# Two-layer trunk on one core: where the residual sum at each layer's end is made (matrix unit with the identity, scalar engine and GpSimd, in place of vector engine adds)

## The chip, the cores and the metric

The kernel runs on 1 core of one Trainium2 chip. The metric is the device time of one execution in microseconds (us); three runs of the kernel before gave a median of 1525.57 us. Engines are called as the profile calls them: PE is TensorE, DVE is VectorE, ACT is ScalarE, POOL is GpSimd, SP is SyncE; PSUM is PE's output memory of 8 banks, each 128 rows of 512 f32 values.

## The reference, cut to what matters

```python
D_MODEL, SEQ, DEPTH, N_EXPERTS, TOP_K = 1024, 512, 2, 16, 2
ALPHA = (2.0 * DEPTH) ** 0.25

def moe(x, ...):
    e_idx, gates = route(xf, w_router, b_router)      # top 2 of 16 experts per token
    ...
    hb = jax.nn.silu(xb @ w1[e]) * (xb @ w3[e])       # one expert on its tokens
    y = (hb @ w2[e]) * gate
    out = jnp.zeros((t, d), x.dtype).at[tok_s].add(y) # two shares per token
    return out.reshape(bsz, seq, d)

for layer in range(DEPTH):
    m = conv_mixer(x, ...) if layer % 2 == 0 else rglru_mixer(x, ...)
    x = layer_norm(ALPHA * x + m, ln1_g[layer], ln1_b[layer])
    f = moe(x, w_router, b_router, moe_w1[layer], moe_w3[layer], moe_w2[layer])
    x = layer_norm(ALPHA * x + f, ln2_g[layer], ln2_b[layer])
```

The change lies in the last line, `layer_norm(ALPHA * x + f)`, which is run twice: at the end of layer 0 (here "the first end", about 704 to 755 us into the execution) and at the end of layer 1 ("the last end", from about 1460 us to the end of the program).

## The kernel before, in words

The 512 tokens are four tiles of 128 rows (`NT` = 4), each row 1024 wide. Every weight matrix is brought in raw pieces (`raw`, 1 MB each) and split for PE into a high part `wh` (ACT, L137) and a low part `wl` (DVE, in places POOL, L148); a product is then three matmuls, high by high, high by low and low by high (L305). An expert runs w1, w3 and w2 in four steps each. Between w3 and w2 its hidden rows are transposed on PE in two halves (L271, `turn(0)` and `turn(1)`); each half is taken out of its bank as a high part `ht0h`, `ht1h` (ACT, L418) and a low part `ht0l`, `ht1l` (DVE, L421).

All engines work through their own queues in the order in which the code is written, and that order is written out by hand in `moe`. `ws.later` collects the low parts of the weight piece that is taken meanwhile, and `ws.lows()` writes them: for the last expert this puts the low part of the piece for w2(1) as four 128x512 instructions on DVE between `ht0l` and `ht1l`.

The experts before the last one scatter their gated rows to DRAM, two shares per token (`yd`). The last expert doesn't. Its end runs like this:

- `base_begin`, in the last expert's w1: POOL's queue loads for each tile t the rows of x (`az`, 512 KB, L1486) and the two stored shares (`ay`, 1 MB, L1488). The `az` of two tiles share one buffer. Behind the eight loads POOL adds the two shares, one 128x1024 add for each tile (L1491).
- `base_sum(t)`: DVE makes `az = ALPHA * az + ay` (128x1024, L1496): tile 0 between the two last `wl` pieces, tiles 1 to 3 behind `yl`.
- w2 gives two halves of 512 columns: w2(0) and w2(1) the first, w2(2) and w2(3) the second. `share(h)` takes half h out, times the gate, as `yh` (ACT, L1502) and `yl` (DVE, L1503).
- `total_mm(t, h)`: PE puts the last expert's rows at their tokens' places in a bank, by two matmuls with the one-hot matrix `place` (L1509).
- `total_half(t, h)`: DVE adds the bank to `az` (128x512, L1516) and takes the norm's statistics of the sum (`bn_stats`, L1517).
- `total(t)` does the second half so and then the moments: two small DVE instructions (L547, L548) and the power -1/2 on POOL (L549).

Then, at the first end, ACT normalises each tile (L1676, after a small DVE instruction, L1673), PE transposes it (L563) and DVE takes the transposes out (L577), which is the input of layer 1's first product. At the last end ACT normalises (L1768), gain and bias are put on by POOL for columns 0 to 383 and by DVE for the rest (L1772, L1773), and the rows leave by SP's queue.

Lines to follow in the code: L1480 to L1491 (`base_begin`), L1493 to L1497 (`base_sum`), L1506 to L1522, and the last expert's part of `moe`.

Of the kernel before, what the change touches and what calls it, by code (L numbers as in the profile page):

```python
# [15 lines left out]
AF = mybir.ActivationFunctionType  # L16
OP = mybir.AluOpType
AX = mybir.AxisListType

P = 128  # L20
T = 512
NT = T // P
# [7 lines left out]
ALPHA = 4.0 ** 0.25  # L30
# [317 lines left out]
class Trunk:  # L348
# [1002 lines left out]
    def moe(self, layer, loaded):  # L1351

        nc, tc, ws = self.nc, self.tc, self.ws
        v = nc.vector
        slots, hot = {}, []

        def aux(q):
            return lambda t: self.aux[:, t, q]

        def fill(qs, hot):  # L1360
            slots.update(zip(qs, self.slot_rows(hot, [aux(q) for q in qs], [q in SMALL for q in qs])))

        hot0 = self.one_hot(self.pos[:, :, 0])
        first = self.slot_rows([hot0], [aux(0)], [False], ())
        rows = self.R("in", "xe")
        nc.gpsimd.memset(rows, 0.0)
        xe = self.gather((first[0][:, 0:1],), False, rows)
        ws.lows()
        self.rank()
        ws.open, ws.total, ws.cap = True, True, 32  # L1370
        ws.pump()
        nxt = Block(self, ws, plain=True)
        nxt.rows_in(xe)
        self.choice()
        self.placed()
        nxt.w1(0)
        hot = [self.one_hot(self.pos[:, :, q], v, q in SMALL) for q in (1, 2, 3)]
        nxt.rest()
        nxt.w1(1)
        self.gates_out()  # L1380
        nxt.w1(2)
        nxt.w1(3)
        slots[0], = self.slot_rows([hot0], [aux(0)], [False], first)
        fill([1, 2, 3], hot)
        hot = []
        xe = self.gather(slots[1], 1 in SMALL, rows)
        for e in range(E):
            cur, last = nxt, e == E - 1
            if e < 12:
                q = e // 4 * 4 + 4 + 2 * (e % 4)  # L1390
                if e % 4 < 2:
                    hot += [self.one_hot(self.pos[:, :, i], nc.gpsimd, i in SMALL) for i in (q, q + 1)]
                if e % 4 == 2:
                    q = e // 4 * 4 + 4
                    fill(list(range(q, q + 4)), hot)
                    hot = []
            if e == E - 2:
                ws.cap = 16
            if e:
                cur.w1(1)  # L1400
                cur.w1(2)
                if last:
                    self.base_begin()
                cur.w1(3)
            cur.w3(0)
            if e == 1:
                self.extra_blocks()
            if e == 4:
                self.nextra = nc.values_load(self.ni[0:1, 0:1], min_val=0, max_val=32)
            cur.w3(1)  # L1410
            cur.w3(2)
            if not last:
                nxt = Small(self, ws) if e + 1 in SMALL else Block(self, ws, 4 if e == E - 2 else 2)
                nxt.rows_in(xe)
                if e + 2 < E:
                    xe = self.gather(slots[e + 2], e + 2 in SMALL, rows)
            ws.later = []
            cur.w3(3)
            cur.turn(0)
            ws.lows()  # L1420
            if last:
                cur.turn(1)
            else:
                nxt.w1(0, ws.next(), lambda h: h or cur.turn(1))
                ws.ahead()
            cur.w2(0)
            if last:
                loaded()
                self.base_sum(0)
            cur.w2(1)  # L1430
            if e == E - 2:
                self.place_rows(slots[E - 1][0])
            if last:
                break
            cur.w2(2)
            cur.w2(3)
            self.scatter(cur.ys, slots.pop(e), cur.small, ROOM[e])
            if e == E - 2:
                with tc.If(self.nextra > 0):  # L1439
                    it = self.S([P, 1], F32, "it", bufs=1)  # L1440
                    nc.vector.memset(it, 0.0)
                    self.kept = {}
                    with tc.For_i(0, self.nextra, 1):
                        self.extra(layer, it)
                    self.kept = None
        gate = slots[E - 1][1]
        self.share(0, cur.ys[0], gate)
        for t in (1, 2):
            self.base_sum(t)
        ws.lead = 1  # L1450
        cur.w2(2)
        self.base_sum(3)
        ws.lead = 0
        for t in range(NT):
            self.total_mm(t, 0)
        cur.w2(3)
        for t in range(2):
            self.total_half(t, 0)
        self.share(1, cur.ys[1], gate)
        for t in range(2):  # L1460
            self.total_mm(t, 1)
        for t in range(2, NT):
            self.total_half(t, 0)
            self.total_mm(t, 1)
        ws.total, ws.open, ws.cap = False, False, 10
        ws.lead = 4
        ws.later = []
        ws.ahead()
# [11 lines left out]
    def base_begin(self):  # L1480

        nc = self.nc
        self.bz, self.bp, self.yhl, self.bst = [], {}, {}, {}
        for t in range(NT):
            z = self.V([P, D], F32, "az")
            nc.gpsimd.dma_start(z, self.x1d[t * P:(t + 1) * P])  # L1486
            y = self.V8([P, 2, D], F32, "ay")
            nc.gpsimd.dma_start(y, self.yd[2 * t * P:2 * (t + 1) * P].rearrange("(p k) d -> p k d", k=2))  # L1488
            self.bz.append((z, y))
        for _, y in self.bz:  # L1490
            nc.gpsimd.tensor_tensor(y[:, 0], y[:, 0], y[:, 1], op=OP.add)  # L1491

    def base_sum(self, t):  # L1493

        z, y = self.bz[t]
        self.nc.vector.scalar_tensor_tensor(z, z, ALPHA, y[:, 0], op0=OP.mult, op1=OP.add)  # L1496
        self.bz[t] = z  # L1497

    def share(self, h, ps, gate):
# [3 lines left out]
        self.nc.vector.scalar_tensor_tensor(lo, ps, gate, hi.bitcast(F32), op0=OP.mult, op1=OP.subtract)  # L1503
        self.yhl[h] = (hi, lo)

    def total_mm(self, t, h):  # L1506
        ps = self.bp[t, h] = self.bank()
        for i, q in enumerate(self.yhl[h]):
            self.nc.tensor.matmul(ps, self.place[:, t * P:(t + 1) * P], q, start=(i == 0), stop=(i == 1))  # L1509

    def total_half(self, t, h):

        if h == 0:
            self.bst[t] = self.S([P, 2, 6], F32, "bst", bufs=4)
        z = self.halves(self.bz[t])[h]
        self.nc.vector.tensor_tensor(z, z, self.bp.pop((t, h)), op=OP.add)  # L1516
        self.nc.vector.bn_stats(self.bst[t][:, h], z)  # L1517

    def total(self, t):

        self.total_half(t, 1)
        return self.halves(self.bz[t]), self.moments(self.bst.pop(t))  # L1522

    def extra(self, layer, it):

# [277 lines left out]
```

## Time and profile before

| | |
|---|---|
| median of 3 runs | 1525.57 us (1524.83 to 1527.47) |
| the profiled execution's own time | 1530.19 us |
| its span, first to last instruction | 1528.4 us |
| mean granted PE clock over the span | 0.959 |
| PE, DVE, ACT, POOL busy | 91%, 74%, 51%, 28% of the span |
| HBM | 469.50 MB read, 29.62 MB written |

The span is cut by nature into the mixers and the two expert stages. In the expert stages the transfers take about 420 GB/s for long stretches; at each layer's end there is nothing left of the experts' weights to load, and the engines finish what is there. The profile's rows are single executions: a sum made from them stands against 1530.19 us, not against the median. A row of the timeline gives an instruction's start, its length, engine, line and what it writes and reads; a length includes time in which the instruction was held, so the same instruction can stand there with 1.2 us and with 3.4 us. The granted clock of PE is 1.00 at 2.4 GHz and 0.50 at 1.2 GHz.

### The profile page before, as it was taken

What the parts mean: (1) busy time and instruction counts of PE and PEld (TensorE: products, weight loads), DVE (VectorE), ACT (ScalarE), POOL (GpSimd) and SP (SyncE); (2) the same over time, 40 slices, a digit from 0 to 9 for tenths busy, and PEclk for the clock granted to TensorE, in tenths of its full rate; (3) what the DMA queues carried; (4) which work ended last, traced back from release to release, by engine and by line L of the source; (5) the groups of instructions that cost most, each with busy time, mean ns of one, the idle gap of its engine ahead of it and who ended that gap; (6) DMA issues with size and microseconds to landing.
All of it is one profiled execution on the core that took longest, in us unless ns stands there. A gap on an engine that the chain in (4) does not pass through costs nothing. (4 is left out here: it accounts for less than half of the span.)

```text
span 1528.4 us, 18167 instructions
## 1 busy us (share of the span) xinstructions
PE 1396.3 (91%) x6456; PEld 1026.4 (67%) x6456; DVE 1126.9 (74%) x1242; ACT 772.2 (51%) x718; POOL 432.9 (28%) x370
## 2 busy tenths in 40 slices
PE   8999959999999999999689798699999999999972
PEld 7877738677586775677577677485776858665851
DVE  6997788668484774478989987885866748554886
ACT  3543227466473755376546421373755747554741
POOL 3983015204202400003384312250051015000043
PEclk9999979999999999999799999799999999999995
DMA  9645748999999999988823258399999999999771
GB/s 282 219 193 193 286 186 310 392 419 417 420 415 413 421 414 420 420 355 330 228 70 93 94 206 318 144 365 406 421 419 420 410 416 421 415 420 419 286 311 55
DMA packets 120837, 490.71 MB, mean 321 GB/s; under 512 B 14078, under 2 KB 53502, under 8 KB 70564
## 3 DMA queue, kind: packets, MB, share of 16 engines
q1 hardware_dynamic: 102240, 437.29, 72.6%
q0 software_dynamic: 11808, 35.28, 5.9%
q10 hardware_dynamic: 6692, 16.91, 3.0%
q8 instruction: 53, 0.87, 0.2%
q14 instruction: 44, 0.36, 0.1%
HBM read 469.50 MB, written 29.62 MB: 327 GB/s over the span
## 5 line engine op out<-in xcount | busy, mean ns | idle before, releaser
L148 DVE TENSOR_TENSOR wl<-raw,wh 128x2048 fp32r<-128x2048 f32 (+2 forms) x310 | 630.1, 2075 | 242.0 <-ACT wh L137 210.4
L137 ACT ACTIVATE wh<-raw 128x2048 fp32r<-128x2048 f32 (+1 forms) x312 | 535.2, 1757 | 110.3 <-PE p L305 27.0
L305 PE MATMUL p<-wh,xe 128*128 128x512 f32 x1344 | 347.6, 396 | 1.0 <-PEq L1439 0.8
L305 PEld LDWEIGHTS p<-wh,xe 128*128 128x128 f32 x1344 | 248.8, 189 | 56.9 <-issue 7.0
L305 PE MATMUL p<-wl,xe 128*128 128x512 f32 x672 | 187.9, 391 | 3.5 <-DVE wl L148 3.5
L1346 POOL DMA_INDIRECT yd<-y,io x30 | 30.8, 1026 | 497.1 <-ACT y L1344 199.3
L305 PEld LDWEIGHTS p<-wl,xe 128*128 128x128 f32 x672 | 126.0, 188 | 32.3 <-DVE wl L148 5.2
L226 PE MATMUL b<-raw,xs 128*64 128x512 f32 x640 | 146.2, 598 | 0.0
L1278 POOL TENSOR_SCALAR S<-c,posp 128x128 bf16<-128x128 bf16 x96 | 127.0, 1337 | 0.5
L596 PE MATMUL b<-xT,wh 128*128 128x512 f32 (+1 forms) x320 | 119.2, 379 | 6.0 <-ACT wh L137 6.0
L597 PE MATMUL b<-xT,wh 128*128 128x512 f32 (+1 forms) x320 | 118.5, 377 | 3.0 <-DVE xT L421 3.0
L1331 POOL DMA_INDIRECT xe<-x1d,ii x32 | 37.3, 1167 | 291.9 <-PE b L271 138.4
L226 PEld LDWEIGHTS b<-raw,xs 128*64 128x64 f32 x640 | 42.4, 136 | 75.0 <-issue 69.6
L148 POOL TENSOR_TENSOR wl<-raw,wh 128x1024 fp32r<-128x1024 f32 x28 | 71.3, 2555 | 29.3 <-ACT wh L137 14.9
L599 PE MATMUL b<-xT,wl 128*128 128x512 f32 (+1 forms) x320 | 73.5, 373 | 3.8 <-DVE wl L148 3.8
L596 PEld LDWEIGHTS b<-xT,wh 128*128 128x128 f32 x320 | 62.3, 195 | 17.7 <-ACT wh L137 7.6
L597 PEld LDWEIGHTS b<-xT,wh 128*128 128x128 f32 x320 | 62.2, 194 | 13.8 <-DVE xT L421 3.6
L226 PE MATMUL b<-raw,hts 128*64 128x512 f32 x320 | 70.9, 595 | 0.0
L599 PEld LDWEIGHTS b<-xT,wl 128*128 128x128 f32 x320 | 56.9, 191 | 14.3 <-DVE wl L148 4.2
L1344 ACT ACTIVATE y<-p,sg 128x512 f32<-128x512 f32 x40 | 25.3, 685 | 75.4 <-PE p L305 75.4
L761 DVE SCALAR_TENSOR_TENSOR b<-av,c,b 128x510 f32<-128x510 f32 (+27 forms) x87 | 59.8, 731 | 2.2 <-ACT b L754 1.3
L326 DVE TENSOR_TENSOR hs<-hs,p 128x512 f32<-128x512 f32 x44 | 30.2, 685 | 39.6 <-PE p L305 39.6
(309 smaller groups left out, 1913.4 us busy)
## 6 DMA issues: line engine op xcount, KB each, us to landing
raw<-in_moe_w_dram SPq DMA_DIRECT2D x384, 1024.0 KB, 15.3
raw<-in_even_w_in_dram SPq DMA_DIRECT2D x20, 512.0 KB, 7.5
yd<-zero ACTq DMA_DIRECT2D x8, 1024.0 KB, 5.0
ay<-yd POOLq DMA_DIRECT2D x8, 1024.0 KB, 15.0
raw<-in_odd_w_in_dram SPq DMA_DIRECT2D x16, 512.0 KB, 7.5
raw<-in_even_w_out_dram SPq DMA_DIRECT2D x8, 512.0 KB, 8.5
x1d<-z POOLq DMA_DIRECT2D x8, 512.0 KB, 7.6
az<-x1d POOLq DMA_DIRECT2D x8, 512.0 KB, 12.2
```

Of the source, the lines that this page charges most:

```text
L137: self.k.nc.scalar.activation(wh, raw, AF.Copy)
L148: self.lo[0].tensor_tensor(wl, raw, wh.bitcast(F32), op=OP.subtract)
L226: self.nc.tensor.matmul(ps[64 * h:64 * h + 64], stat[i], w[0][:, i, h * HALF:(h + 1) * HALF], start=(first and i == 0), stop=(last and i = ...
L305: self.nc.tensor.matmul(pss[j], stat[i][a], q[:, i, j * HALF:(j + 1) * HALF], start=(first and i == 0 and a == 0 and q is wh), stop=(last ...
L326: self.nc.vector.tensor_tensor(self.hm[h], self.hm[h], self.p3[h], op=OP.mult)
L596: nc.tensor.matmul(ps, ah, bh, start=(i == 0), stop=False)
L597: nc.tensor.matmul(ps, ah, bl, start=False, stop=False)
L599: nc.tensor.matmul(ps, al, bh, start=False, stop=(i == n - 1))
L761: nc.vector.scalar_tensor_tensor(o[:, s:], av[:, 0:T - s], prm[:, i, 30 - s:31 - s], acc[:, s:], op0=OP.mult, op1=OP.add)
L1278: (eng or self.nc.vector).tensor_scalar(S[:, t], self.iota2 if small else self.iota, pos[:, t:t + 1], None, op0=OP.is_equal)
L1331: self.nc.gpsimd.indirect_dma_start(out=xe, out_offset=None, in_=self.by_half(self.x1d) if small else self.x1d[:, :], in_offset=bass.Indir ...
L1346: nc.gpsimd.indirect_dma_start(out=self.by_half(self.yd) if small else self.yd[:, :], out_offset=bass.IndirectOffsetOnAxis(ap=slot[2], axi ...
```

## The change

At both ends the residual sum is made elsewhere. A new `base_add`, written between w3(3) and `turn(0)` of the last expert, lets ACT multiply the x rows of tiles 0 and 1 by ALPHA, and POOL add the two shares of each tile and, for tiles 0 and 1, add that to the x rows: six POOL adds in place of four, and two 128x1024 instructions on ACT. DVE keeps `base_sum` for tiles 2 and 3, now behind both of the last `wl` pieces and `yl`. A new `base_mm(t, h)` lets PE bring each sum into a bank with the identity (f32, 128x512, eight for each end); `total_mm` adds the last expert's rows in the same bank, and `bn_stats` and ACT's normalising read the bank. The eight DVE adds of L1516 for each end are gone.

```diff
--- before.py
+++ after.py
@@ -1416,6 +1416,8 @@
                     xe = self.gather(slots[e + 2], e + 2 in SMALL, rows)
             ws.later = []
             cur.w3(3)
+            if last:
+                self.base_add()
             cur.turn(0)
             ws.lows()
             if last:
@@ -1426,7 +1428,6 @@
             cur.w2(0)
             if last:
                 loaded()
-                self.base_sum(0)
             cur.w2(1)
             if e == E - 2:
                 self.place_rows(slots[E - 1][0])
@@ -1445,23 +1446,27 @@
                     self.kept = None
         gate = slots[E - 1][1]
         self.share(0, cur.ys[0], gate)
-        for t in (1, 2):
-            self.base_sum(t)
         ws.lead = 1
         cur.w2(2)
+        ws.lead = 0
+        for t in range(2):
+            for h in range(2):
+                self.base_mm(t, h)
+        self.base_sum(2)
+        cur.w2(3)
         self.base_sum(3)
-        ws.lead = 0
-        for t in range(NT):
+        self.base_mm(2, 0)
+        self.base_mm(2, 1)
+        for t in range(3):
             self.total_mm(t, 0)
-        cur.w2(3)
-        for t in range(2):
-            self.total_half(t, 0)
+        self.base_mm(3, 0)
+        self.total_mm(3, 0)
         self.share(1, cur.ys[1], gate)
-        for t in range(2):
-            self.total_mm(t, 1)
-        for t in range(2, NT):
-            self.total_half(t, 0)
-            self.total_mm(t, 1)
+        self.total_mm(0, 1)
+        self.total_mm(1, 1)
+        self.base_mm(3, 1)
+        self.total_mm(2, 1)
+        self.total_mm(3, 1)
         ws.total, ws.open, ws.cap = False, False, 10
         ws.lead = 4
         ws.later = []
@@ -1487,8 +1492,17 @@
             y = self.V8([P, 2, D], F32, "ay")
             nc.gpsimd.dma_start(y, self.yd[2 * t * P:2 * (t + 1) * P].rearrange("(p k) d -> p k d", k=2))
             self.bz.append((z, y))
-        for _, y in self.bz:
+
+    def base_add(self):
+
+        nc = self.nc
+        for z, _ in self.bz[:2]:
+            nc.scalar.activation(z, z, AF.Copy, scale=ALPHA)
+        for t, (z, y) in enumerate(self.bz):
             nc.gpsimd.tensor_tensor(y[:, 0], y[:, 0], y[:, 1], op=OP.add)
+            if t < 2:
+                nc.gpsimd.tensor_tensor(z, z, y[:, 0], op=OP.add)
+                self.bz[t] = z
 
     def base_sum(self, t):
 
@@ -1503,23 +1517,23 @@
         self.nc.vector.scalar_tensor_tensor(lo, ps, gate, hi.bitcast(F32), op0=OP.mult, op1=OP.subtract)
         self.yhl[h] = (hi, lo)
 
+    def base_mm(self, t, h):
+
+        ps = self.bp[t, h] = self.bank()
+        self.nc.tensor.matmul(ps, self.ident, self.halves(self.bz[t])[h], start=True, stop=False)
+
     def total_mm(self, t, h):
-        ps = self.bp[t, h] = self.bank()
+
+        ps = self.bp[t, h]
         for i, q in enumerate(self.yhl[h]):
-            self.nc.tensor.matmul(ps, self.place[:, t * P:(t + 1) * P], q, start=(i == 0), stop=(i == 1))
-
-    def total_half(self, t, h):
-
+            self.nc.tensor.matmul(ps, self.place[:, t * P:(t + 1) * P], q, start=False, stop=(i == 1))
         if h == 0:
             self.bst[t] = self.S([P, 2, 6], F32, "bst", bufs=4)
-        z = self.halves(self.bz[t])[h]
-        self.nc.vector.tensor_tensor(z, z, self.bp.pop((t, h)), op=OP.add)
-        self.nc.vector.bn_stats(self.bst[t][:, h], z)
+        self.nc.vector.bn_stats(self.bst[t][:, h], ps)
 
     def total(self, t):
 
-        self.total_half(t, 1)
-        return self.halves(self.bz[t]), self.moments(self.bst.pop(t))
+        return [self.bp.pop((t, h)) for h in range(2)], self.moments(self.bst.pop(t))
 
     def extra(self, layer, it):
 
```

The order of instructions on the engines, at the last end (the first end has the same). First DVE: `ht0l`, `ht1l` are the low parts of the transposed hidden rows, `wl` the low parts of the weights, `yl` the low part of the last expert's output. Before:

```order
L421 TENSOR_TENSOR ht0l_11591<-b_11585,ht0h_11590 128x512
L148 TENSOR_TENSOR wl_11569<-raw_11496,wh_11568 128x512 x4
L421 TENSOR_TENSOR ht1l_11604<-b_11598,ht1h_11603 128x512
L148 TENSOR_TENSOR wl_11610<-raw_11520,wh_11609 128x2048
L1496 SCALAR_TENSOR_TENSOR az_11474<-az_11474,ay_11476 128x1024
L148 TENSOR_TENSOR wl_11631<-raw_11538,wh_11630 128x2048
L1503 SCALAR_TENSOR_TENSOR yl_11647<-p_11607,sg_10084,yh_11646 128x512
L1496 SCALAR_TENSOR_TENSOR az_11474<-az_11474,ay_11479 128x1024
L1496 SCALAR_TENSOR_TENSOR az_11481<-az_11481,ay_11483 128x1024
L1496 SCALAR_TENSOR_TENSOR az_11481<-az_11481,ay_11486 128x1024
L1516 TENSOR_TENSOR az_11474<-az_11474,b_11665 128x512
L1517 BN_STATS bst_11689<-az_11474 128x6
```

And now:

```order
L421 TENSOR_TENSOR ht0l_11597<-b_11591,ht0h_11596 128x512
L148 TENSOR_TENSOR wl_11567<-raw_11494,wh_11566 128x512 x4
L421 TENSOR_TENSOR ht1l_11610<-b_11604,ht1h_11609 128x512
L148 TENSOR_TENSOR wl_11616<-raw_11518,wh_11615 128x2048
L148 TENSOR_TENSOR wl_11636<-raw_11536,wh_11635 128x2048
L1517 SCALAR_TENSOR_TENSOR yl_11652<-p_11613,sg_10086,yh_11651 128x512
L1510 SCALAR_TENSOR_TENSOR az_11483<-az_11483,ay_11485 128x1024
L1510 SCALAR_TENSOR_TENSOR az_11483<-az_11483,ay_11488 128x1024
L1532 BN_STATS bst_11695<-b_11667 128x6
L1532 BN_STATS bst_11699<-b_11671 128x6
L1532 BN_STATS bst_11703<-b_11689 128x6
```

The sums of tiles 0 and 1 are gone from DVE, the sum of tile 0 no longer stands between the last two `wl`, and behind `yl` stand two sums and then statistics that read banks, with no adds.

ACT at the turn, with the semaphores that each row waits for (DMASW: a transfer issued by POOL's queue). `ht0h` and `ht1h` are the high parts of the transposed rows. Before:

```order
L137 ACTIVATE wh_11568<-raw_11496 128x2048 [waits DMAHW5_49,DVE_49,PE_49]
L418 ACTIVATE ht0h_11590<-b_11585 128x512 [waits PE_49]
L418 ACTIVATE ht1h_11603<-b_11598 128x512 [waits PE_49,Pool_49]
L137 ACTIVATE wh_11609<-raw_11520 128x2048 [waits DMAHW6_49,DVE_49]
L137 ACTIVATE wh_11630<-raw_11538 128x2048 [waits DMAHW7_49,DVE_49]
L1502 ACTIVATE yh_11646<-p_11607,sg_10084 128x512 [waits PE_49]
```

And now:

```order
L137 ACTIVATE wh_11566<-raw_11494 128x2048 [waits DMAHW5_49,DVE_49,PE_49]
L1500 ACTIVATE az_11476<-az_11476 128x1024 [waits DMASW2_49,DMASW0_49]
L1500 ACTIVATE az_11476<-az_11476 128x1024 [waits DMASW2_49]
L418 ACTIVATE ht0h_11596<-b_11591 128x512 [waits PE_49]
L418 ACTIVATE ht1h_11609<-b_11604 128x512 [waits PE_49]
L137 ACTIVATE wh_11615<-raw_11518 128x2048 [waits DMAHW6_49,DVE_49]
L137 ACTIVATE wh_11635<-raw_11536 128x2048 [waits DMAHW7_49,DVE_49]
L1516 ACTIVATE yh_11651<-p_11613,sg_10086 128x512 [waits PE_49]
```

Two multiplications of 128x1024 stand ahead of `ht0h`; the first of them waits for two transfers of x rows, which share a buffer.

POOL, from the last load of shares to the first power. Before:

```order
L1488 DMA ay_11486<-yd_997 128x2048
L1491 TENSOR_TENSOR ay_11476<-ay_11476 128x1024
L1491 TENSOR_TENSOR ay_11479<-ay_11479 128x1024
L1491 TENSOR_TENSOR ay_11483<-ay_11483 128x1024
L1491 TENSOR_TENSOR ay_11486<-ay_11486 128x1024
L549 TENSOR_TENSOR mv_11719<-mv_11719,c_426 128x1
```

And now:

```order
L1493 DMA ay_11488<-yd_997 128x2048
L1502 TENSOR_TENSOR ay_11478<-ay_11478 128x1024
L1504 TENSOR_TENSOR az_11476<-az_11476,ay_11478 128x1024
L1502 TENSOR_TENSOR ay_11481<-ay_11481 128x1024
L1504 TENSOR_TENSOR az_11476<-az_11476,ay_11481 128x1024
L1502 TENSOR_TENSOR ay_11485<-ay_11485 128x1024
L1502 TENSOR_TENSOR ay_11488<-ay_11488 128x1024
L549 TENSOR_TENSOR mv_11729<-mv_11729,c_426 128x1
```

Between the adds of shares of tiles 0, 1 and 2 stand two adds to the x rows.

## Rows read from the trace of the kernel before

**Rows 1.** The page's first line: the span.

```profile
span 1528.4 us, 18167 instructions
```

**Rows 2.** The chain of work that ended last, at the last end, in order of time: start, us, engine, what it writes, line.

```profile
1483.63 4.42 DVE wl L148
...
1488.77 3.35 PE b L1509 x7
1492.12 4.06 PE p L305 x12
...
1506.83 1.35 POOL z L1772
```

**Rows 3.** The timeline of DVE at the first end: start, us, engine, line, operation, out<-in with shapes, count.

```profile
715.66 2.49 DVE L148 TENSOR_TENSOR wl<-raw,wh 128x512 fp32r<-128x512 f32 x4
718.06 0.68 DVE L421 TENSOR_TENSOR ht1l<-b,ht1h 128x512 fp32r<-128x512 f32 x1
...
722.47 1.21 DVE L1496 SCALAR_TENSOR_TENSOR az<-az,ay 128x1024 f32<-128x1024 f32 x1
723.61 4.43 DVE L148 TENSOR_TENSOR wl<-raw,wh 128x2048 fp32r<-128x2048 f32 x1
727.96 0.74 DVE L1503 SCALAR_TENSOR_TENSOR yl<-p,sg,yh 128x512 fp32r<-128x512 f32 x1
728.62 4.99 DVE L1496 SCALAR_TENSOR_TENSOR az<-az,ay 128x1024 f32<-128x1024 f32 x3
```

**Rows 4.** The timeline of POOL at the first end; in brackets the idle time ahead of a row and what ended it.

```profile
717.95 2.45 POOL L1491 TENSOR_TENSOR ay<-ay 128x1024 f32<-128x1024 f32 x1 [2.73 <-DMA ay<-yd]
722.73 3.16 POOL L1491 TENSOR_TENSOR ay<-ay 128x1024 f32<-128x1024 f32 x1 [2.33 <-DMA ay<-yd]
727.38 2.88 POOL L1491 TENSOR_TENSOR ay<-ay 128x1024 f32<-128x1024 f32 x1 [1.49 <-DMA ay<-yd]
741.56 0.57 POOL L549 TENSOR_TENSOR mv<-mv,c 128x1 f32<-128x1 f32 x1 [11.30 <-DVE mv L548]
...
746.96 0.55 POOL L549 TENSOR_TENSOR mv<-mv,c 128x1 f32<-128x1 f32 x1 [1.27 <-DVE mv L1673]
```

**Rows 5.** The timeline of ACT at the first end, and what it did with pieces of 128x1024.

```profile
714.42 0.60 ACT L418 ACTIVATE ht0h<-b 128x512 fp32r<-128x512 f32 x1 [2.88 <-PE b L271]
...
736.21 3.89 ACT L137 ACTIVATE wh<-raw 128x1024 fp32r<-128x1024 f32 x4
```

**Rows 6.** Transfers issued at 703.9 to 704.7 and at 1459.89 to 1460.4: KB each and us from issue to landing. The `az` in each is that of tile 1.

```profile
az<-x1d POOLq DMA_DIRECT2D x1, 512.0 KB, 10.7
...
az<-x1d POOLq DMA_DIRECT2D x1, 512.0 KB, 9.6
```

**Rows 7.** The timeline of POOL at the last end, from the first add of shares.

```profile
1467.52 3.69 POOL L1491 TENSOR_TENSOR ay<-ay 128x1024 f32<-128x1024 f32 x1 [4.41 <-DMA ay<-yd]
...
1478.60 4.02 POOL L1491 TENSOR_TENSOR ay<-ay 128x1024 f32<-128x1024 f32 x1 [3.38 <-DMA ay<-yd]
...
1502.14 0.57 POOL L549 TENSOR_TENSOR mv<-mv,c 128x1 f32<-128x1 f32 x1 [16.24 <-DVE mv L548]
```

**Rows 8.** The timeline of DVE at the last end.

```profile
1472.29 0.69 DVE L421 TENSOR_TENSOR ht0l<-b,ht0h 128x512 fp32r<-128x512 f32 x1 [0.41 <-ACT ht0h L418]
1472.90 4.67 DVE L148 TENSOR_TENSOR wl<-raw,wh 128x512 fp32r<-128x512 f32 x4
1477.49 0.68 DVE L421 TENSOR_TENSOR ht1l<-b,ht1h 128x512 fp32r<-128x512 f32 x1
...
1500.23 0.67 DVE L1516 TENSOR_TENSOR az<-az,b 128x512 f32<-128x512 f32 x1
1500.94 0.69 DVE L1517 BATCH_NORM_STATS2 bst<-az 128x6 f32<-128x512 f32 x1
```

**Rows 9.** The timeline of PE: one row of the last end, then two of the first end.

```profile
1475.29 1.07 PE L305 MATMUL p<-wh,ht1h 128*128 128x512 f32 x4
...
728.76 0.79 PE L1509 MATMUL b<-yl,place 128*128 128x512 f32 x1 [4.71 <-DVE yl L1503]
...
733.61 1.07 PE L305 MATMUL p<-wh,ht1l 128*128 128x512 f32 x4
```

**Rows 10.** Stretches of time, busy us (and instructions) of PE, its granted clock, the transfers' share and GB/s. The first two are of all engines: PE, PEld, DVE, ACT, POOL, then the clock; the third is of L305 alone, the fourth of L296 alone, an f32 product of 128x128 by 128x512.

```profile
724.10:728.70 4.60, 0.00 (x0) 0.00 (x0) 4.60 (x3) 0.00 (x0) 3.11 (x2) 0.79 1.08 325
...
1489.00:1494.50 5.50, 5.50 (x14) 4.24 (x15) 5.43 (x7) 0.00 (x0) 0.00 (x0) 0.50 0.00 0
...
1480.17:1482.89 2.72, 2.72 (x13) 1.00 0.48 200
...
219.00:226.00 7.00, 7.00 (x18) 1.00 0.45 150
```

**Rows 11.** The norm's statistics by source: from a bank (L541, in the mixer) and from SBUF (L1517), ns least/median/most, first and last start.

```profile
L541 DVE BATCH_NORM_STATS2 bst<-b x4: 690/692/692, 135.4 to 147.9; 128x6 f32<-128x512 f32 x4
...
L1517 DVE BATCH_NORM_STATS2 bst<-az x16: 694/694/697, 734.2 to 1507.9; 128x6 f32<-128x512 f32 x16
```

**Rows 12.** What stands behind the statistics: DVE at the first end, then POOL's last row of the program.

```profile
747.54 2.30 DVE L1673 SCALAR_TENSOR_TENSOR mv<-mv 128x1 f32<-128x1 f32 x1 [0.60 <-POOL mv L549]
749.77 2.79 DVE L577 TENSOR_SCALAR xv<-b,c 128x256 f32<-128x256 f32 x6
...
1517.97 0.99 POOL L1773 TENSOR_TENSOR z<-z,b 128x384 f32<-128x384 f32 x1
```

## The prediction

> **What bounds the kernel now.** I read the span [rows 1], then the chain of waits at the last end [rows 2], then the timelines of DVE, POOL, ACT and PE at both ends, each change standing there twice. The chain goes from a DVE weight split held at 4.42 us (1483.63) over PE's placing (3.35 us for seven matmuls) and its last twelve products (4.06 us) through DVE's adds and statistics to POOL's first gain at 1506.83 [rows 2]. So an end is a relay of DVE, PE and DVE, and no transfer is waited for after the shares. Two things to see on the way.
>
> First, DVE and POOL hold each other up. POOL's add at 722.73 is listed with 3.16 us, DVE's sum at 722.47 with 1.21 and DVE's next split at 723.61 with 4.43 [rows 3, 4]: the sum runs to 723.68, POOL then to 725.89 (2.2 us), the split from there to 728.04. DVE's split stood ready behind the sum, and POOL came in between all the same. It goes on so: POOL's add of 727.38 runs when that split ends, to 730.26, and DVE's three sums, ready at 728.62, take 4.99 us of which 1.6 are waiting [rows 3, 4]. Whoever waits gets the next turn, for a whole instruction. DVE's work on banks (`ht1l`, 0.68; `yl`, 0.74) is not stretched [rows 3].
>
> By the Trainium skill (SBUF — State Buffer, Who interferes with whom) a DVE instruction with two SBUF inputs and a POOL instruction that reads SBUF exclude each other for a whole instruction; the rows agree, and it says nothing of who comes next.
>
> Second, PE's clock. PE idles for 4.7 us until 728.76 [rows 9], and its granted clock falls within that idle time (mean 0.79) and is 0.50 in 1489.0 to 1494.5, where PE works after the like wait of the last end [rows 10]. 0.50 is 1.2 GHz. At the first end PE is back at its pace (1.07 us for four) at 733.61 [rows 9]: about 4.9 us of work at half speed, 2.4 us lost.
>
> **The change part by part.** Durations: an ACT pass over 128x1024 is 3.89/4 = 0.97 us [rows 5], 1.0 with its wait. A POOL add is 2.2 us when it runs alone, a quarter split on DVE 2.49/4 = 0.62 [rows 3]. Statistics from a bank take 691 ns, from SBUF 694 [rows 11]: reading banks costs nothing.
>
> *ACT's two multiplications.* They stand ahead of `ht0h` and wait for the x rows of tile 1, which land at 703.9 + 10.7 = 714.6 and 1459.9 + 9.6 = 1469.5 [rows 6]. At the first end they end at 716.7, and `ht0h` was at 714.42 [rows 5]: 2.3 us later. At the last end they end at 1471.5, and `ht0l` was taken out by 1472.98 [rows 8], after ACT's part of 0.6: no cost. Behind them on ACT stand both halves' evictions and the last two `wh` splits; PE's w2 waits for the former, and the splits come 2.3 later at the first end, still ahead of DVE's low parts.
>
> *POOL's two more adds meet the four quarter splits.* Before, `ht1l` followed the four quarters, at 718.06 and 1477.49 [rows 3, 8], and only one POOL add was in their way (none at the first end; at the last end 4.67 instead of 2.49 us). Now POOL has adds queued through that whole time. Replayed with the rule of turns. First end: sum to x of tile 0 at 715.7 to 717.9; `ht0l` 717.3 to 718.0; quarter to 718.6; shares of tile 1 (there at 717.95 [rows 4]) to 720.8; quarter to 721.4; sum of tile 1 to 723.6; quarter to 724.2; shares of tile 2 (there at 722.73) to 726.5; quarter to 727.1; `ht1l` done at 727.8, before 718.74: **9.1 us later**. Last end: POOL's first add ends at 1471.21 [rows 7], so sum 0 to 1473.5; quarter to 1474.1; shares 1 to 1476.3; quarter to 1476.9; sum 1 to 1479.2; quarter to 1479.8; shares 2 (there at 1478.60 [rows 7]) to 1482.0; quarter to 1482.6; `ht1l` done at 1483.3, before 1478.17: **5.1 us later**.
>
> By the Trainium skill (Perfetto Trace Analysis, Optimizing Scalar/DVE Operations) moving work from DVE to GpSimd might not help, as the two share a read port. Here two sums of 1.2 us on DVE become two POOL adds of 2.2, and that rule would give what the replay gives.
>
> *PE from `ht1l` to the first statistics.* It has run out of work at 1476.2, one step after 1475.29 [rows 9], and about 721 at the first end: 7 us of idle time in each, more than the waits before which the clock fell. What follows is 34 of the split products and placings at 2.72/12 = 0.227 us [rows 10] (8 of w2(1), 12 of w2(2), 12 of w2(3), 2 of tile 0's placing), 7.7; six identity products, which I cost by L296, 0.43 at most (18 records touch 7.00 us) [rows 10], 2.6; 0.2 for the handover; and a half-speed stretch. That one I take at 5.8 us of work, between the 4.9 above and 6.7, so 2.9 lost (2.4 to 3.4). Sum 13.4: first statistics at 741.2 and 1496.7; before, DVE took its first statistics at 734.25 (first start of L1517 [rows 11]) and, by the chain, after the seven placings (1492.12 [rows 2]) and one 0.67 add, 1492.8. So +7.0 and +3.9. PE's second idle time, until `yl`, goes: both last splits end within w2(2) and w2(3). The banks that the sums now hold until ACT has normalised them cost nothing: a half's transposes need four banks and wait for the same two tiles anyway.
>
> *The adds that go.* Behind the first statistics DVE had eight pairs of add and statistics, 0.71 + 0.70 apart [rows 8]; now eight statistics, banks being full. From first statistics to POOL's last power it was 746.96 - 734.25 = 12.7 at the first end [rows 4, 11]. Now: 4 x 0.62 for the first halves, 0.72 for `yl`, 0.46 for two placings, 4 x 0.66, then 0.4 to the first power: 6.7. Before, the first power came 741.56 - 734.25 = 7.3 after, nearly the same, but then only tile 0 was done; now the other three powers follow 0.55 apart, the last 8.4 us after the first statistics. **4.3 us back.**
>
> *What each end comes to.* First end: last power at 749.6 against 746.96, +2.6; DVE's first transposes came 749.77 - 746.96 = 2.8 behind [rows 4, 12] and should again, at 752.4. ACT's four normalisings now run in a row from 748.6 and put the second half's transposes 3.3 later. I take **+3.0** (-0.4 to +4). The next layer starts from there, so all of it counts. Last end: first power at 1503.4 against 1502.14 [rows 7], normalised tile at 1505.5, POOL's first gain behind DVE's share of it at 1506.4 against 1506.83 [rows 2], -0.4. The rest, 12.1 us from there to 1518.96 [rows 2, 12], is DVE and POOL in turns on gains and biases; it loses the statistics that stood between, some 0.4. **-0.8** (-2.5 to +2).
>
> Sum +2.2 on 1530.19, 1532.4. The profiled execution lies 4.62 above the median of 1525.57; the change carries over as it is: **1527.8**, the forecast's own range -2 to +5, 1523.5 to 1530.5.
>
> **Rivals.** *Quarters in one run (faster).* If DVE's four quarters, which have no waits between them, keep POOL out until they end, `ht1l` is done at 1476.6 and 721.0. For it: no row shows POOL coming between instructions as short. Against: at 723.68 it came in before a split that was ready. Then POOL's adds collide with the two large splits and the two sums instead; in turns, the first statistics come at about 1491.6 and 735.9, and with the 4.3 back the last end gains 5 and the first 2, of which a short half-speed stretch takes 1: -6, **1519.6** (1517 to 1523).
>
> *PE at half speed for longer (slower).* The idle time of 7 us is longer than both seen, and PE may work 10 us at 1.2 GHz: 5.0 lost instead of 2.9, +2.1 at each end, first end +5.1, last +1.3: +6.4, **1532.0**. It decides once the first statistics start after 743 and 1498. With all 13 us at half speed (0.45 and 0.85 each) it is 6.5 more at each end, the outer bound.
>
> *No net shift (same).* The first end's delay could be taken up in layer 1, where PE waits for other things: then only the last end's -0.8 stays, **1524.8**.
>
> **How the numbers follow.** Forecast 0.57, quarters together 0.24, longer half speed 0.13, taken up 0.06. A change of 0.2%, 3.05 us, is about what a measurement of this kernel can tell from none. Within it lie 0.37 of the forecast's cases, 0.03 of the second, all of the last: 0.46. Faster: 0.21 of the second and 0.02 of the forecast: 0.23. Slower: 0.18 of the forecast and the third's 0.13: 0.31. The range 1519 to 1533 leaves out about half of the fast rival and the outer bound.
>
> **What would show it.** In the profile after: POOL adds alternating with the quarter splits, listed at 2 to 3 us each, and `ht1l` at about 727 and 1482.6 (right), or at 720.3 and 1476 (the fast rival); PE idle about 7 us ahead of it and a granted clock of 0.50 behind; first statistics at 741 and 1497; four powers 0.55 apart; DVE's first transposes at 752 to 753. The prediction is wrong if the quarters run together, if the identity products take far from 0.43, or if layer 1 starts no later.

## The result, and the profile after

The changed kernel took **1534.43 us** (median of 7 runs, 1529.79 to 1535.95) against 1525.57 us before (7 runs, 1524.43 to 1527.96): ratio **1.0054, interval 1.0041 to 1.0067**, 8.2 us slower by the ratio. The forecast said +2.2, that is 1527.8, with a range of 1519 to 1533: the direction is right, the size is not. The first profile of the changed kernel is of its fastest run, 1529.79 us. Two more profiles help to read it: one of the changed kernel (1538.52 us, the slowest of the six runs timed with it) and one of the kernel before (1523.74 us). They show how far one execution lies from the next, which the single trace ahead of the prediction couldn't; the two profiles of the changed kernel are the two extremes.

This is DVE at the last end of the changed kernel, first profile, the answer to [rows 8]:

```profile
1465.72 1.42 DVE L326 TENSOR_TENSOR hs<-hs,p 128x512 f32<-128x512 f32 x2
1468.14 0.69 DVE L421 TENSOR_TENSOR ht0l<-b,ht0h 128x512 fp32r<-128x512 f32 x1 [1.00 <-ACT ht0h L418]
1468.75 10.61 DVE L148 TENSOR_TENSOR wl<-raw,wh 128x512 fp32r<-128x512 f32 x4
1479.28 0.68 DVE L421 TENSOR_TENSOR ht1l<-b,ht1h 128x512 fp32r<-128x512 f32 x1
...
1495.96 1.89 DVE L1532 BATCH_NORM_STATS2 bst<-b 128x6 f32<-128x512 f32 x3 [6.50 <-PE b L1529]
```

The four quarters take 10.61 us where they took 4.67 before and 2.49 undisturbed. POOL in the same time, the answer to [rows 7]:

```profile
1468.12 2.42 POOL L1504 TENSOR_TENSOR az<-az,ay 128x1024 f32<-128x1024 f32 x1
1470.50 2.82 POOL L1502 TENSOR_TENSOR ay<-ay 128x1024 f32<-128x1024 f32 x1
1473.39 2.67 POOL L1504 TENSOR_TENSOR az<-az,ay 128x1024 f32<-128x1024 f32 x1
1476.03 2.79 POOL L1502 TENSOR_TENSOR ay<-ay 128x1024 f32<-128x1024 f32 x1
```

Four adds, each listed with 0.2 to 0.6 us more than the 2.2 of one alone: a quarter goes between every two of them, as the replay had it. PE, the answer to [rows 9]:

```profile
1480.01 2.08 PE L305 MATMUL p<-wh,ht1l 128*128 128x512 f32 x4 [7.92 <-DVE ht1l L421]
...
1487.42 3.59 PE L1523 MATMUL b<-az,c 128*128 128x512 f32 x8
1490.45 1.48 PE L305 MATMUL p<-wh,ht1h 128*128 128x512 f32 x4
1491.78 1.07 PE L305 MATMUL p<-wh,ht1l 128*128 128x512 f32 x4
...
1493.59 1.88 PE L1523 MATMUL b<-az,c 128*128 128x512 f32 x4
1494.90 0.79 PE L1529 MATMUL b<-yh,place 128*128 128x512 f32 x1
1495.54 0.39 PE L1529 MATMUL b<-yl,place 128*128 128x512 f32 x1
```

PE idles 7.92 us and then works at half pace (2.08 us for four products, granted clock 0.50 in the stretch 1479.70 to 1485.30 below). The surprise is L1523: the order has four identity products there and the trace eight records, 3.03 us from the first to what follows, **0.76 us for a product**. And the first product of the other kind behind them takes longer: 1.33 us from start to start for four at 1490.45 (0.90 at 1491.78 to 1492.68), 0.64 for the first placing at 1494.90 (0.23 for the next).

```profile
1479.70:1485.30 5.60, 5.29 (x13) 4.13 (x13) 5.60 (x3) 0.69 (x1) 3.57 (x1) 0.50 0.00 1
```

To compare executions I take times from the end of DVE's second `hs` add (L326) of the last expert, 1467.14 in the rows above; each is a difference of two starts or ends in the timelines. At the first end: `ht1l` done, first statistics, DVE's first transposes (L577). At the last end: `ht1l`, first statistics, POOL's first gain, POOL's last instruction.

| profile | first end | last end |
|---|---|---|
| before, first profile | 4.4, 19.9, 35.4 | 6.3, 20.9, 35.0, 47.1 |
| before, second profile | 4.4, 19.9, 35.7 | 6.7, 20.6, 32.4, 44.5 |
| changed, first profile | 10.9, 24.3, 36.4 | 12.8, 28.8, 38.2, 51.5 |
| changed, second profile | 12.8, 29.0, 41.1 | 12.8, 29.0, 38.3, 51.6 |

The last end is 4.4 to 7.1 us longer, the first 0.7 to 5.7. In the changed kernel it is the first end that differs between the two profiles, in the kernel before the last.

### The profile page after: what moved, and what is told of

Its sections match the earlier page's. It is cut to its first block, busy times and chain, and to the rows that moved or that the text cites. A ratio compares the mean times of both kernels' runs of the same rounds, so it can differ in the third digit from the quotient of the medians.

```text
span 1528.0 us, 18218 instructions
## 1 busy us (share of the span) xinstructions
PE 1409.0 (92%) x6488; PEld 1032.6 (68%) x6488; DVE 1116.4 (73%) x1222; ACT 774.8 (51%) x722; POOL 442.3 (29%) x374
## 5 line engine op out<-in xcount | busy, mean ns | idle before, releaser
L148 DVE TENSOR_TENSOR wl<-raw,wh 128x2048 fp32r<-128x2048 f32 (+2 forms) x310 | 643.4, 2118 | 240.1 <-ACT wh L137 223.0
L305 PE MATMUL p<-wh,xe 128*128 128x512 f32 x1344 | 346.5, 395 | 0.8 <-PEq L1440 0.7
L305 PEld LDWEIGHTS p<-wh,xe 128*128 128x128 f32 x1344 | 247.9, 188 | 56.4 <-issue 7.0
L305 PE MATMUL p<-wl,xe 128*128 128x512 f32 x672 | 187.3, 390 | 2.0 <-DVE wl L148 2.0
L305 PEld LDWEIGHTS p<-wl,xe 128*128 128x128 f32 x672 | 125.8, 188 | 30.6 <-DVE wl L148 3.6
L597 PEld LDWEIGHTS b<-xT,wh 128*128 128x128 f32 x320 | 62.9, 197 | 12.9 <-DVE xT L421 2.9
L305 PE MATMUL p<-wh,ht1l 128*128 128x512 f32 x176 | 48.2, 396 | 11.0 <-DVE ht1l L421 11.0
```

Source lines behind the costliest of these rows:

```text
L148: self.lo[0].tensor_tensor(wl, raw, wh.bitcast(F32), op=OP.subtract)
L305: self.nc.tensor.matmul(pss[j], stat[i][a], q[:, i, j * HALF:(j + 1) * HALF], start=(first and i == 0 and a == 0 and q is wh), stop=(last ...
L597: nc.tensor.matmul(ps, ah, bl, start=False, stop=False)
```

## The experiments

Theory A: turns. The added POOL adds hold DVE's quarters, so `ht1l` and PE come late. Theory B: the loss lies between the ends. Theory C: the identity products cost far more than my sum has. The runs below were made on three chips; each ratio is to the kernel before on the same chip.

### The changed kernel and the kernel before once more

No edit.

> The changed kernel once more, timed and with a second profile. Theory A (turns: the added POOL adds hold DVE's four quarter splits, ht1l and PE wait, all of the loss lies in the two ends): 1533 to 1536 us, and in this trace the two ends together are 6 to 9 us longer than in the second profile of the kernel before, the quarters listed with 7 to 11 us. Theory B (the loss lies mostly between the ends, in layer 1 or its loads): the ends together are 2 to 5 us longer and the rest of the 8 us stands between them. Theory C (identity products: 0.76 us each in the first profile against 0.43 in my sum, 8 in each end): the quarters matter less, and from ht1l to the first statistics PE is busy 2 us longer than my 13.4.

> The kernel before as its own rival: ratio 1.000 within 0.001 by every theory; its second profile shows how far an end's length (from the last expert's hs to DVE's first transposes, and to the end of the program) moves from one execution to the next. I expect under 1 us for each end and 2 to 4 us for the whole.

The changed kernel: 1533.36 us, ratio 1.0061 (1.0039 to 1.0083). The kernel before: ratio 1.0000 (0.9985 to 1.0015). The ends in the changed kernel's second profile are together 12.5 us longer than in the second of before (5.4 and 7.1). That is above the 6 to 9 that A expected. B isn't needed: outside the two ends the span is 1445.9 and 1441.7 us in the two profiles of before, 1440.1 and 1444.1 in those of the changed kernel. Over all profiles but that of the run without identity products this rest lies between 1440.1 and 1449.6, so from one execution to the next it moves by more than the change costs, and a single profile's own time says little. My expectation that an end moves by under 1 us between executions was wrong: the last end of before moved by 2.6, the first of the changed kernel by 4.7. These are DVE at the first end of the changed kernel, first the first profile and then the second:

```profile
714.54 7.37 DVE L148 TENSOR_TENSOR wl<-raw,wh 128x512 fp32r<-128x512 f32 x4
```

```profile
717.16 9.60 DVE L148 TENSOR_TENSOR wl<-raw,wh 128x512 fp32r<-128x512 f32 x4
726.68 0.68 DVE L421 TENSOR_TENSOR ht1l<-b,ht1h 128x512 fp32r<-128x512 f32 x1
```

One turn of 2.2 us lies between them. In the first, POOL's add of the shares of tile 1 came up in the middle of the quarters and was listed with 2.93 us, two quarters having run ahead of it; in the second it started at once. PE then idled 3.1 us in the one and worked on at a clock of 1.00; in the other it idled 6.9 us and went on at 0.50. The length of that idle time doesn't settle the pace by itself: at the last end of the second profile of before PE idled 2.00 us until 1474.73 and its next products took 1.91 us for four. The kernel before has turns of the like: POOL's last add at the last end came at 1483.42, ahead of the split that is listed from 1483.63 with 4.42 us [rows 2]; in its second profile it came 1.0 us after that split had begun, which took 2.28 us. The turn then fell into the three sums behind `yl` (5.01 us against 3.48), and PE waited less for `yl`. First the split in the second profile, then PE's wait for `yl` in the first and in the second:

```profile
1480.10 2.28 DVE L148 TENSOR_TENSOR wl<-raw,wh 128x2048 fp32r<-128x2048 f32 x1
```

```profile
1488.77 0.79 PE L1509 MATMUL b<-yl,place 128*128 128x512 f32 x1 [5.49 <-DVE yl L1503]
```

```profile
1483.10 0.50 PE L1509 MATMUL b<-yl,place 128*128 128x512 f32 x1 [1.70 <-DVE yl L1503]
```

### The low part in one instruction

```diff
-        elif big:
+        elif big and n != 4:
             self.later += [(wl[:, i], raw[:, i], wh[:, i]) for i in range(n)]
```

> The changed kernel with the low part of the w2(1) piece written as one 128x2048 instruction and not as four quarters, so that POOL can come in once and not three or four times. Theory A: ht1l comes 3 us earlier at the first end and 6 at the last, and the time falls 3 to 6 us against the changed kernel, to 1528 to 1531. Theory B: no more than 2 us less. Theory C: no more than 1 us less, since PE's own work sets the end.

1527.40 us, ratio 1.0019 (1.0006 to 1.0033): 6 us less than the changed kernel. The instruction is held once:

```profile
1468.43 4.11 DVE L148 TENSOR_TENSOR wl<-raw,wh 128x2048 fp32r<-128x2048 f32 x1
1472.46 0.68 DVE L421 TENSOR_TENSOR ht1l<-b,ht1h 128x512 fp32r<-128x512 f32 x1
```

`ht1l` is done 6.2 us after `hs` instead of 12.8, and the last end is 6.4 us shorter (45.2). At the last end A is right that the number of places where POOL can come in is what costs. At the first end `ht1l` is done after 6.1, and yet DVE's first transposes come at 36.4, as in the first profile of the changed kernel: PE now waits for DVE's sum of tile 2 instead, 2.77 us there and as long at the last end:

```profile
1487.10 1.95 PE L1523 MATMUL b<-az,c 128*128 128x512 f32 x4 [2.74 <-DVE az L1510]
```

### All four sums back on DVE

`base_add` isn't called, POOL's four adds stand in `base_begin` as before, and `base_sum(0)` and `base_sum(1)` on DVE: the first at its old place, the second behind `yl`.

> The changed kernel with the sums of tiles 0 and 1 back on DVE at their old places and POOL with its four adds as before; the identity products, the banks and the statistics from them stay. Theory A: ht1l is back at its old place and the time at 1524 to 1527, 0 to 2 us of gain against the kernel before. Theory B: the same as the changed kernel within 3 us. Theory C: 1528 to 1532, as the identity products stay.

1532.92 us, ratio 1.0058 (1.0036 to 1.0079): as slow as the changed kernel, so A alone falls. `ht1l` is back at 4.4 and 6.6, but PE, at the first end, stands still (3.50 us at the last end):

```profile
723.73 1.98 PE L1525 MATMUL b<-az,c 128*128 128x512 f32 x4
731.36 3.78 PE L1525 MATMUL b<-az,c 128*128 128x512 f32 x4 [5.65 <-DVE az L1512]
```

Tile 1's identity products wait for DVE's sum of tile 1 ahead of w2(3), and after the wait run at half pace. One wait had taken the place of another.

### The same, with tile 1's products behind w2(3)

```diff
-        for t in range(2):
-            for h in range(2):
-                self.base_mm(t, h)
+        for h in range(2):
+            self.base_mm(0, h)
         self.base_sum(2)
         cur.w2(3)
+        for h in range(2):
+            self.base_mm(1, h)
```

> The kernel with all four sums on DVE (1532.9 us), and with tile 1's identity products put behind w2(3), so that PE no longer waits for tile 1's sum ahead of w2(3) (5.65 and 3.5 us in the trace). If that new wait is what kept it slow: 3 to 5 us less, 1528 to 1530. If the price of the identity products is: 1531 to 1533, as before.

1529.46 us, ratio 1.0011 (0.9993 to 1.0030): 3.5 to 7 us less (by medians, by ratios), the two intervals lying apart. The wait of 5.65 us is gone (2.12 are left), and the ends are 5.5 and 4.3 us shorter: that wait was the cause there.

### No identity products

```diff
-        for t in range(2):
-            for h in range(2):
-                self.base_mm(t, h)
...
-        ps = self.bp[t, h]
+        ps = self.bp[t, h] = self.bank()
...
-            self.nc.tensor.matmul(ps, self.place[...], q, start=False, stop=(i == 1))
+            self.nc.tensor.matmul(ps, self.place[...], q, start=(i == 0), stop=(i == 1))
```

> The changed kernel without the identity products, so that the output lacks alpha x and the stored shares; ACT's, POOL's and DVE's sums are still made. Theory A (turns alone; identity products near the 0.43 us of my sum): 4 to 5 us less than the changed kernel, 1528 to 1530, quarters and ht1l as late as before. Theory C (0.76 us each, and some 0.4 us at each change of kind on PE, 7 to 8 us in each end): 10 to 14 us less, 1519 to 1523.

The kernel leaves alpha x and the stored shares out of its sums. The time (1953.58 us) says nothing: layer 1 gets other rows, routes other tokens to its experts, and runs other blocks. Only the first end can be read, and there `ht1l` is as late as in the changed kernel's second profile (12.9 against 12.8), so the two are alike up to that point:

```profile
727.36 2.07 PE L305 MATMUL p<-wh,ht1l 128*128 128x512 f32 x4 [7.04 <-DVE ht1l L421]
...
736.33 0.39 PE L1522 MATMUL b<-yh,place 128*128 128x512 f32 x1
736.56 0.39 PE L1522 MATMUL b<-yl,place 128*128 128x512 f32 x1
```

First statistics 22.5 us after `hs` instead of 29.0, first transposes 33.6 instead of 41.1: 7.5 us less at that end. Of these, 1.3 lie ahead of the first product: from its first work on `ht1l` to the end of w2(2) PE took 6.25 us against 7.57, its half pace having ended earlier; why it did isn't shown. That leaves 6.2 for the eight products with their changes of kind. To have a time as well, I left them out at the last end alone, behind which nothing is routed (`if self.layer == 0` ahead of the product).

> The changed kernel without the identity products at the last end alone, where the output then lacks alpha x and the stored shares; nothing of the routing depends on it. Price of eight products as the first end showed it in the trace without them (ht1l as late as ever, first statistics 6.4 and first transposes 7.5 us earlier): 6 to 8 us less than the changed kernel, 1525 to 1528. If the turns alone make the last end late: 2 to 4 us less, 1529 to 1532.

1529.18 us, ratio 1.0017 (0.9998 to 1.0035): some 0.4% or 6 us less than the changed kernel by the ratios, near the low end of what C gave. The absolute time alone doesn't decide: 1529.18 lies in the range that I had set for the turns alone, the kernel before having taken 1526.52 on that chip. The trace decides. With `ht1l` still at 12.8, the last end is 43.9 long, 7.6 less than with them (again 1.3 of it in PE's half pace). C is right as well.

### ACT's and POOL's sums alone, in the kernel before

`base_add` as in the change, `base_sum` for tiles 2 and 3 only; DVE's adds of L1516 stay, no identity products.

> The kernel before with only the sums of tiles 0 and 1 moved to ACT and POOL at their new place; DVE still adds the banks, no identity products. Theory A: the four quarters are listed with 7 to 11 us as in the changed kernel, ht1l comes 5 to 8 us later, of which PE's old wait for yl takes back some: 1527 to 1531. Theory C: within 1 us of the kernel before.

1532.52 us, ratio 1.0036 (1.0019 to 1.0054). These sums alone, turns and ACT's multiplications together, make the kernel before 5.5 us slower. Its quarters at the last end (those of the first take 9.68):

```profile
1474.87 10.76 DVE L148 TENSOR_TENSOR wl<-raw,wh 128x512 fp32r<-128x512 f32 x4
1485.56 0.68 DVE L421 TENSOR_TENSOR ht1l<-b,ht1h 128x512 fp32r<-128x512 f32 x1
```

### The change at the last end alone

`moe` takes the old code for layer 0 and the new for layer 1.

> The change at the last end alone; the first end as in the kernel before. From the traces of the changed kernel, the last end is 5 to 7 us longer and the first 1 to 5.5. If the two ends carry the whole loss: 1529 to 1532 on a kernel before of 1524 to 1526, 4 to 7 us slower. If the loss lies in layer 1 between them (the first end's delay growing on its way): 0 to 3 us slower.

1533.16 us, ratio 1.0046 (1.0032 to 1.0061), 7.0 us. The last end carries most of the loss; some 1 us, which lies within the intervals, is left for the first.

### Another order

The kernel with the one low part, and PE's order at the end written anew: tiles 0 and 1 are placed in full as soon as w2(3) is done, ahead of the products with the sums of tiles 2 and 3, the first of which PE waited for above.

```diff
         cur.w2(3)
-        self.base_sum(3)
-        self.base_mm(2, 0)
-        self.base_mm(2, 1)
...
         self.share(1, cur.ys[1], gate)
+        for h in range(2):
+            for t in range(2):
+                self.total_mm(t, h)
+        self.base_sum(3)
+        for t in (2, 3):
+            for h in range(2):
+                self.base_mm(t, h)
+            for h in range(2):
+                self.total_mm(t, h)
...
```

> The changed kernel with the low part in one instruction, and with PE placing both halves of tiles 0 and 1 right behind w2(3), ahead of the sums of tiles 2 and 3 that it waits for; the second share is taken out there too. If what is left to the kernel before (about 3 us) is PE's and DVE's waiting for one another at the end (2.7 us for the sum of tile 2 and 1.2 us for yl in each end), it gains 3 to 6 us on the kernel with the one low part: 1521 to 1525. If PE's own work sets the end: 1526 to 1528.

1522.94 us, ratio 0.9980 (0.9965 to 0.9996): faster than both kernels. First end 32.9, last 43.4. Then the last end's moments of all tiles were written ahead of the first normalising:

```diff
-    todo, zs = [], {}
+    todo, zs = [k.total(t) for t in range(NT)], {}
     for t in range(NT + 2):
-        if t < NT:
-            todo.append(k.total(t))
```

> The reordered changed kernel with the last end's moments of all four tiles written ahead of the first normalising, so that POOL's fourth power no longer stands behind two gains of DVE. The tail from POOL's first gain to its last instruction, 13.3 us in the changed kernel against 12.1 before, should fall by about 1 us: 1521 to 1523, 0 to 1.5 us less than the reordered kernel. If the turns of POOL and DVE set the tail: no change within 0.5 us.

1521.96 us, ratio **0.9970** (0.9952 to 0.9988). POOL's tail from its first gain to its end goes from 13.3 to 11.9 us, as expected; the gain on the kernel with the other order alone lies within the intervals. And the order without the change:

> The kernel before, without identity products, ACT and POOL sums, but with what helped the changed kernel: the low part in one instruction, the sum of tile 0 behind yl, the second share right behind w2(3), tiles 0 and 1 placed and added before 2 and 3. If the order alone makes the gain of the reordered changed kernel: 1520 to 1523. If the banks and the identity do, since DVE keeps its eight adds: 1524 to 1527.

1523.74 us, ratio 0.9979 (0.9961 to 0.9998), here without a change in where the sums are made. The kernel before gets as much from the one low part and the order as the changed kernel, and the banks and identity products add nothing that can be seen. Its last end shows that the cuts mattered even there: `ht1l` is done 4.2 us after `hs`, 6.3 and 6.7 before.

## Why the prediction was wrong in size

**The turns: right.** *POOL's two more adds meet the four quarter splits* gave `ht1l` 9.1 and 5.1 us later; measured against the second profile of before it is 8.4 (second profile of the changed kernel; 6.4 in the first) and 6.2. The fast rival, *quarters in one run*, is out: the quarters are listed with 7.4 to 10.8 us in every profile that has POOL's adds there.

**ACT's two multiplications: nearly right.** They took 1.05 us each. `ht0h` came 1.3 to 1.6 us later behind `hs` at the first end (forecast 2.3) and 0.3 to 0.6 at the last (forecast none); both are inside the times of `ht1l`.

**PE's idle time and half speed: right at the last end.** 7.9 us of idle time there against 7, then 0.50. At the first end it was so in the second profile (6.9 us); in the first PE idled 3.1 us and kept its pace. The longer half speed of the slow rival didn't come: PE is at full pace from 1486.50 on, some 6 us, where I took 5.8.

**The identity products: the step that failed.** *PE from `ht1l` to the first statistics* came out at 13.4 us, and was 16.2 at both ends of the second profile and 16.0 at the last end of the first. I costed a product at 0.43 by L296, "18 records touch 7.00 us". An f32 product leaves two records: the program's order has 32 instructions of L296 where the trace has 64 records, and 16 of L1523 with 32:

```profile
L1523 PE MATMUL b<-az,c x32: 590/592/592, 727.4 to 1500.9; 128*128 128x512 f32 x32
```

So a product is 0.76 us, 0.33 more than I took, 2.0 for the six ahead of the first statistics; the two changes from identity products to split products and placings add 0.4 each, 0.8, which my sum had at nothing. That makes 16.2. Without the eight the ends were 7.5 and 7.6 us shorter, 6.2 and 6.3 of it the products' own, where 0.43 each would have made 3.4. At the first end of the first profile the time is 13.4 us, as forecast, by luck: the 2.8 more for the products stand against the 2.9 of half speed that didn't come there. By the Trainium skill (FP8 and Floating Point Precision, TensorE Precision Notes) a true FP32 product is four passes; by the split product's 0.227 that would be an estimate of 0.91, and the trace has 0.76, 3.3 times: nearer to it than my 0.43.

**The adds that go: right in kind, too large.** Statistics from banks took 690 ns. From first statistics to POOL's first gain it is 9.3 us where I had 9.7. But the baseline was one execution: 14.1 us in the first profile of before, 11.8 in its second, since the turn at 1483.63, PE's long wait for `yl` and its half pace behind it fell into the first alone. Of the 4.4 us that I counted back at the last end, 2.3 were that, and against the second profile 2.5 came back. At the first end 3.4 to 3.7 came back between first statistics and transposes, where the forecast has 4.0 (from +7.0 to +3.0).

**The tail: wrong.** I took 0.4 off the 12.1 us behind POOL's first gain; it became 13.3. The chain of waits of the changed kernel (start, us, engine, what it writes, line) shows how:

```profile
1505.89 1.08 DVE z L1786
...
1507.00 1.50 DVE z L1787
...
1508.50 0.13 DVE mv L547
...
1508.88 1.13 POOL mv L549
...
1510.02 1.30 POOL z L1786
```

The fourth tile's moments (L547) stand behind DVE's gain and bias of tile 0, and POOL's power (L549) and its next gain wait for them. With the moments ahead the tail is 11.9.

Last end, measured less forecast, second profiles: `ht1l` +1.1, from there to the first statistics +3.4 (2.8 of it the identity products), to the first gain +1.9, the tail +1.5. Sum 7.9, which with the forecast's -0.8 is the 7.1 that the last end grew by, and 7.0 is what the run with the last end alone gave. The identity products are the largest single part of the miss, the baseline and the tail make most of the rest. The first end was forecast at +3.0 and is 0.7 to 5.7, by the runs some 1: the turns there depend on which of two things comes first by some tenths of a microsecond.

**Not settled.** How often the first end takes the one course or the other. The run without the products at the last end alone has the changed kernel's first end, and took the short course there: quarters of 7.35 us, transposes at 36.3. The run without any products and the kernel before with the sums on ACT and POOL took the long one up to `ht1l` (9.71 and 9.68). That is two short and three long, too few to say. For the same reason the rival *no net shift* isn't settled either: what the first end loses is within the noise of the times, and no run shows whether layer 1 takes it up.

## What to carry to other kernels

Where two engines take turns for a whole instruction each, cutting one engine's work into pieces gives the other a place to come in at every cut: count the other engine's instructions that are ready in that time, and keep a chain that others wait for in one piece. Before a price is taken from a row's count, hold the count against the program's instructions, as one may leave several records. And take the baseline from more than one profile where the stretch in question has such turns: from first statistics to POOL's first gain the kernel before took 14.1 us in one and 11.8 in the other.

## What I had not expected of the hardware

An f32 product of 128x128 by 128x512 takes 0.76 us at full clock against 0.227 for a split one, and the first product of the other kind behind it starts its successor 0.4 us later. POOL's waiting add came in between DVE's instructions of 0.62 us, queued back to back without a wait, at nearly every one of the cuts (10.61 us for 2.49 us of work; in the short course two quarters ran first, and it was 7.37).
